# Pinning every engine but TensorE to source order in the seven-product stage of an encoder trunk

## The chip, the cores and the metric

The kernel runs on one core of a Trainium2 chip. The metric is the device time of one execution in microseconds (us). Engines are named as the profile names them: PE (TensorE matmuls), PEld (its weight loads), DVE (VectorE), ACT (ScalarE), POOL (GpSimd, here an issuer of DMAs) and SP (SyncE, which issues the other DMAs).

## The reference

Two requests, 512 and 256 tokens of width 1024 (768 columns together), pass through two layers. A layer is a mixer, a gated feed-forward part and a small embedding gate. The change lies in the feed-forward part, which is, cut short:

```python
def _conv_ffn(x, w_up, conv_w, conv_b, w_down):
    u = x @ w_up                                   # 1024 -> 2 * 2816
    up = jnp.pad(u, ((0, 0), (1, 1), (0, 0)))
    u = up[:, :-2] * conv_w[0] + up[:, 1:-1] * conv_w[1] + up[:, 2:] * conv_w[2] + conv_b
    a, gate = jnp.split(u, 2, axis=-1)
    return (a * jax.nn.gelu(gate, approximate=False)) @ w_down
```

All arithmetic is float32.

## The kernel before

Activations lie transposed: 128 features on the partitions, tokens along the free dimension. Float32 accuracy comes from splitting both operands of a matmul into a rounded high part and the low rest (`hi` by ACT, `lo = x - hi` by DVE), and from three matmuls: high by high, high by low, low by high.

`ffn` runs in three parts. The first 4 of the 22 blocks of 128 inner features are computed in the plain way (`proj`). The other 18 (`for j in range(NSTD, NF)`) form the seven-product stage: a block needs a 2 by 2 product of block matrices (two halves of the inner dimension, two halves of 384 tokens), and `seven` makes it with seven products in place of eight, from sums of weight blocks (S1 to S4) and of activations (N1, N2, T3, N4). The third part multiplies by `w_down`.

One iteration of the stage, in the order of the source (P1 to P7 are the products, twelve matmuls of 384 columns each; "step" is what `split_step` runs after the product):

- P1 = A11 B11. ACT copies it to `q1` (L184). Step: high and low part of S3 of this block.
- P2 = S1 N1. Step: high and low of S1 of the *next* block, then a POOL transfer into the same place.
- P3 = S2 N2. DVE: `u2` = P3 + q1 (L191), `g` = P2 + u2 (L192). Step: high and low of S4 of this block, then SP loads the pair of weight blocks after the next.
- P4 = S3 T3. DVE adds it and `g` into `us[1]` (L1081). Step: A11 of the next block, POOL transfer.
- P5 = A12 B21, summed onto P1's bank. ACT copies it to `us[0]` (L1083). Step: A12 of the next block, and a POOL transfer (L128) for the block after that.
- P6 = S4 B22, summed onto P2's bank, which `g` must have read. DVE adds (L1081). Step: S2 of the next block, POOL transfer.
- P7 = A22 N4, onto P4's bank. DVE adds (L1081). Step: A22 of the next block.

The sums S1, S2, S3, S4 of weights are made by transfers: POOL issues a DMA that adds a block of HBM onto the tile that holds the one before (L115 in `more`, L128). So S1, S2 and S4 of one block come one out of the other in the tile `ra`: load (L88), add, S1, add, S2, add, S4. The tile has two buffers, so the load for block j + 2 waits until S4 of block j is split. The high and low parts of one block pair share `whi` and `wlo` (two buffers), the others use `hs` and `ls` (three).

The convolution and gating of block j (`activate`) run during iteration j + 1: two Identity activations (L1028) at the end of iteration j, then one piece at each of the first five products: gate tap, gate tap, Gelu and a linear tap, a linear tap, and the product (DVE L1031, L1051; ACT L318).

The lines of `seven` on which most turns (`after` runs one piece of the convolution and one split step):

```python
        prod(y, "S2", "N2", True)
        nc.vector.tensor_tensor(out=u2, in0=y, in1=q1, op=ALU.add)
        nc.vector.tensor_tensor(out=g, in0=z, in1=u2, op=ALU.add)
        after()
```

Nothing but data dependences holds this order. A scheduler lays out each engine's instructions by its own estimate of when each is ready, with the source order as priority. Each engine then runs its queue strictly in the order laid out, and waits at the first instruction that isn't ready.

Of the kernel before, what the change touches and what calls it, by code (L numbers as in the profile page):

```python
# [45 lines left out]
class Net:  # L46
# [119 lines left out]
    def seven(self, c11, add):  # L166
        nc = self.nc
        X, W = self.X, self.pw.pop(0)

        def prod(bank, a, b, start):  # L170
            for n, ((wh, wl), (xh, xl)) in enumerate(zip(W[a], X[b])):
                for i, (w, v) in enumerate(((wh, xh), (wh, xl), (wl, xh))):
                    nc.tensor.matmul(bank, w, v, start=start and n == 0 and i == 0, stop=n == 3 and i == 2,  # L173
                                     skip_group_check=True)

        def after():
            self.tick()
            self.split_step()
        q1 = self.rp.tile([128, T], F32, tag="Rt", name="q1")[:, 0:HC]
        ug = self.rp.tile([128, T], F32, tag="sq", name="ug")  # L180
        u2, g = ug[:, 0:HC], ug[:, HC:T]
        x, z = self.mm()[:, 0:HC], self.mm()[:, 0:HC]
        prod(x, "A11", "B11", True)
        nc.scalar.copy(q1, x)  # L184
        after()
        prod(z, "S1", "N1", True)
        self.begin_split()
        after()
        y = self.mm()[:, 0:HC]
# [4 lines that stand above are left out]
        v = self.mm()[:, 0:HC]  # L194
        prod(v, "S3", "T3", True)
        add(1, 1, v, g)
        after()
        prod(x, "A12", "B21", False)
        c11(x)
        after()  # L200
        prod(z, "S4", "B22", False)
        add(0, 1, z, u2)
        after()
        prod(v, "A22", "N4", False)
        add(1, 0, v, u2)
        after()

# [779 lines left out]
    def ffn(self, l):  # L989
        nc, tc, a = self.nc, self.tc, self.a  # L990
        with tc.tile_pool(name=f"f{l}", bufs=1) as fp, \
# [43 lines left out]
            def activate(j, u, negated):  # L1035
                act[j] = aslot(j, f"act{j}", F32)
                if negated:
                    c = self.hp.tile([128, AC], F32, tag="h6", name="cg")
                else:
                    c = self.rp.tile([128, AC], F32, tag="sq", name="cg")  # L1040
                gbias = conv[:, NF + j, 3:4]
                gate = conv_taps(c, u[1], *((nconv, j, gbias) if negated else (conv, NF + j, gbias)))
                lin = conv_taps(act[j], u[0], conv, j, conv[:, j, 3:4])
                next(gate), next(lin)
                yield 1
                for _ in gate:
                    yield 1
                self.other(c, c, AF.Gelu)
                for _ in lin:
                    yield 1  # L1050
                nc.vector.tensor_tensor(out=act[j], in0=act[j], in1=c, op=ALU.mult)  # L1051

            def run(gen):
                for _ in gen:
                    pass
# [5 lines left out]
            for j in range(NSTD):  # L1061
                for part in range(2):
# [9 lines left out]
                    if part == 1:  # L1072
                        run(activate(j, us, False))
            self.drain()
            self.begin_split()
            for _ in range(6):
                self.split_step()
            for j in range(NSTD, NF):
# [6 lines left out]
                next(taps)  # L1085
                self.spawn(taps)
            self.drain()
            self.use_lnexp()
            for ph in range(2):
                accs = []  # L1090
# [281 lines left out]
```

## Time and profile before

| | |
|---|---|
| median of 3 runs | 2441.41 us (2431.51 to 2442.25) |
| the profiled execution, its own time | 2439.16 us |
| its span | 2437.4 us |
| PE busy, mean granted clock | 2313.6 us (95%), 0.981 |
| DVE, ACT, POOL busy | 1459.0, 1036.0, 193.3 us |
| first seven-product stage (layer 0) | 770.6 to 1103.6 us of the span |
| second one (layer 1) | 1814.8 to 2153.7 us of the span |

Busy shares are averages over stages; what the change is worth is read from the two stages. In the rows further down, a time in square brackets is how long the engine sat idle before the instruction and who ended that. The granted clock of PE has two levels, 1.00 (2.4 GHz) and 0.50 (1.2 GHz).

### The profile page before, as it was taken

The numbers are of one execution on the slowest core, as the hardware profiler recorded it, in microseconds if no ns is written. First come the engines' busy times: TensorE is split into PE (matmuls) and PEld (weight loads), VectorE is DVE, ScalarE is ACT, GpSimd is POOL, SyncE is SP. The second block draws the span as 40 slices with busy tenths as digits, with TensorE's granted clock in tenths as the row PEclk, the third lists the DMA queues.
The fourth block names the chain that finished last, engine by engine and source line by source line (L and its number), as shares of the span: only waits on it lengthen the run. The fifth ranks groups of instructions, "written<-read, shape, count | busy, mean of one in ns | idle before, by whom it ended". The sixth has DMA issues, their size and how long they took to land. (4 is left out here: it accounts for less than half of the span.)

```text
span 2437.4 us, 33498 instructions
## 1 busy us (share of the span) xinstructions
PE 2313.6 (95%) x13572; PEld 2098.2 (86%) x13572; DVE 1459.0 (60%) x2172; ACT 1036.0 (43%) x1506; POOL 193.3 (8%) x240
## 2 busy tenths in 40 slices
PE   7999999999999888889999999999998888899997
PEld 6989889898889878888888899998888887788887
DVE  7536364454568666665435687866596566664366
ACT  5333243323445334344335565545353343343353
POOL 1010010100002121110000000000021111200000
PEclk9999999999999999999999999999999999999999
DMA  4111111112336555553222211114265555531221
GB/s 158 52 53 44 53 44 44 52 44 85 110 102 133 117 110 115 109 106 102 67 74 81 97 53 36 41 38 136 100 136 114 108 106 115 101 118 61 74 87 52
DMA packets 85658, 208.74 MB, mean 86 GB/s; under 512 B 9632, under 2 KB 11680, under 8 KB 85504
## 3 DMA queue, kind: packets, MB, share of 16 engines
q1 hardware_dynamic: 60736, 162.03, 20.4%
q0 software_dynamic: 23616, 43.00, 11.7%
q8 instruction: 107, 1.75, 0.3%
q10 hardware_dynamic: 1152, 1.57, 0.2%
q14 instruction: 47, 0.39, 0.0%
HBM read 193.98 MB, written 12.58 MB: 85 GB/s over the span
## 5 line engine op out<-in xcount | busy, mean ns | idle before, releaser
L256 PE MATMUL pj<-xh,whi 128*128 128x512 f32 x2288 | 607.2, 346 | 9.1 <-ACT whi L73 6.0
L256 PE MATMUL pj<-xl,whi 128*128 128x512 f32 x2288 | 587.5, 338 | 3.5 <-DVE xl L312 3.5
L256 PE MATMUL pj<-xh,wlo 128*128 128x512 f32 x2288 | 585.7, 337 | 0.0
L256 PEld LDWEIGHTS pj<-xl,whi 128*128 128x128 f32 x2288 | 352.1, 188 | 56.0 <-DVE xl L312 5.3
L256 PEld LDWEIGHTS pj<-xh,whi 128*128 128x128 f32 x2288 | 351.1, 189 | 52.9 <-ACT whi L73 6.0
L256 PEld LDWEIGHTS pj<-xh,wlo 128*128 128x128 f32 x2288 | 349.7, 188 | 50.7
L73 ACT ACTIVATE whi<-raw 128x1024 fp32r<-128x1024 f32 (+2 forms) x182 | 181.0, 995 | 409.7 <-PE pj L256 391.5
L173 PE MATMUL mm<-x,whi 128*128 128x384 f32 x720 | 218.4, 371 | 93.6 <-DVE ug L192 90.8
L78 DVE TENSOR_TENSOR wlo<-raw,whi 128x1024 fp32r<-128x1024 f32 (+2 forms) x162 | 197.2, 1218 | 145.6 <-ACT whi L73 145.5
L173 PEld LDWEIGHTS mm<-x,whi 128*128 128x128 f32 x720 | 142.5, 207 | 106.4 <-DVE ug L192 101.2
L173 PE MATMUL mm<-x,wlo 128*128 128x384 f32 x432 | 155.5, 360 | 0.0
L110 ACT ACTIVATE whi<-ra 128x512 fp32r<-128x512 f32 x144 | 87.0, 628 | 119.7 <-DMA ra<-w_up 116.9
L173 PE MATMUL mm<-x,hs 128*128 128x384 f32 x432 | 123.0, 339 | 4.9 <-ACT q L184 4.9
L306 DVE TENSOR_TENSOR xl<-act,xh 128x772 fp32r<-128x772 f32 x88 | 83.5, 958 | 68.0 <-ACT xh L305 67.7
L115 POOL DMA_DIRECT2D ra<-w_up x108 | 104.5, 1154 | 245.1 <-DVE ls L111 188.5
L110 ACT ACTIVATE hs<-ra 128x512 fp32r<-128x512 f32 x36 | 22.7, 632 | 221.2 <-DMA ra<-w_up 209.6
L305 ACT ACTIVATE xh<-act 128x772 fp32r<-128x772 f32 x88 | 73.4, 841 | 96.8 <-PE pj L256 93.1
L111 DVE TENSOR_TENSOR ls<-ra,hs 128x512 fp32r<-128x512 f32 x36 | 24.9, 693 | 147.5 <-ACT hs L110 144.0
L111 DVE TENSOR_TENSOR wlo<-ra,whi 128x512 fp32r<-128x512 f32 x144 | 95.9, 687 | 17.3 <-ACT whi L110 16.6
L436 ACT COPY kc<-X 128x768 f32<-128x768 f32 x56 | 50.5, 902 | 124.5 <-PE mm L423 68.2
L173 PE MATMUL mm<-x,ls 128*128 128x384 f32 x288 | 97.1, 337 | 0.0
L111 DVE TENSOR_TENSOR ls<-rb,hs 128x512 fp32r<-128x512 f32 x72 | 49.5, 687 | 78.3 <-ACT hs L110 78.3
(276 smaller groups left out, 4023.7 us busy)
## 6 DMA issues: line engine op xcount, KB each, us to landing
ra<-w_up POOLq DMA_DIRECT2D x144, 256.0 KB, 4.7
raw<-w_ev SPq DMA_DIRECT2D x55, 512.0 KB, 3.5
raw<-w_dn SPq DMA_DIRECT2D x44, 512.0 KB, 3.5
rb<-w_up SPq DMA_DIRECT2D x72, 256.0 KB, 4.1
ra<-w_up SPq DMA_DIRECT2D x72, 256.0 KB, 3.4
raw<-w_od SPq DMA_DIRECT2D x24, 512.0 KB, 3.4
hd<-h SPq DMA_DIRECT2D x24, 384.0 KB, 2.3
h<-hd SPq DMA_DIRECT2D x24, 384.0 KB, 4.0
```

Source lines behind the costliest of these rows:

```text
L73: nc.scalar.activation(hi[:, s], raw[:, s], AF.Copy)
L78: nc.vector.tensor_tensor(out=lo[:, s], in0=raw[:, s], in1=hi[:, s].bitcast(F32), op=ALU.subtract)
L110: nc.scalar.activation(hi, r, AF.Copy)
L111: nc.vector.tensor_tensor(out=lo, in0=r, in1=hi.bitcast(F32), op=ALU.subtract)
L115: nc.gpsimd.dma_start(out=t, in_=src[n], accum_op=ALU.add)
L173: nc.tensor.matmul(bank, w, v, start=start and n == 0 and i == 0, stop=n == 3 and i == 2, skip_group_check=True)
L256: nc.tensor.matmul(o, w, x[:, c0:c0 + n], start=first and si == 0, stop=last and si == 2)
L305: nc.scalar.activation(xh[:, :n], src, AF.Copy)
L306: nc.vector.tensor_tensor(out=xl[:, :n], in0=src, in1=xh[:, :n].bitcast(F32), op=ALU.subtract)
L436: nc.scalar.copy(dst.rearrange("p (n c j) -> p n c j", c=2, j=h), src)
```

## The change

`ffn` notes how many instructions have been traced when the stage begins, and, when its last background work has been traced, calls `in_order`. That goes through the instructions traced between, and ties each to the one before it on the same engine by an edge that orders their issue and makes nothing wait for an end. PE is left out. So DVE, ACT, POOL and SP issue what belongs to the stage in the order of the source. No instruction is added, removed or resized. Work of the parts before and after the stage is not tied, and may still be laid out between.

```diff
+    def in_order(self, start):
+        last = {}
+        for i in list(self.nc.cur_bb.bb.instructions)[start:]:
+            if i.engine == mybir.EngineType.PE:
+                continue
+            if i.engine in last:
+                self.tc.add_manual_dep(i, last[i.engine].name, mybir.DependencyInfo(
+                    mybir.DependencyClass.NoSync, mybir.DependencyReason.DATA), reason="in_order")
+            last[i.engine] = i
...
             self.drain()
+            start = len(nc.cur_bb.bb.instructions)
             self.begin_split()
...
             self.drain()
+            self.in_order(start)
             self.use_lnexp()
```

## Rows read from the trace of the kernel before

**Rows 1.** The page: its span line and the line of engine busy time.

```profile
span 2437.4 us, 33498 instructions
PE 2313.6 (95%) x13572; PEld 2098.2 (86%) x13572; DVE 1459.0 (60%) x2172; ACT 1036.0 (43%) x1506; POOL 193.3 (8%) x240
```

**Rows 2.** Busy time by stretch: length of the stretch, then busy time (and instructions) of each engine, granted clock, mean busy share of the DMA engines, GB/s. The stretches are 170 us before the first stage, the first stage, what follows it, the second stage, and one single iteration.

```profile
600.00:770.00 170.00, 170.00 (x1001) 149.32 (x1000) 112.22 (x147) 80.79 (x111) 21.08 (x32) 1.00 0.41 113
770.60:1103.60 333.00, 284.16 (x1515) 276.59 (x1514) 211.15 (x343) 138.75 (x222) 59.65 (x68) 0.95 0.56 114
1103.60:1500.00 396.40, 396.40 (x2354) 348.98 (x2353) 231.50 (x283) 186.54 (x240) 0.00 (x0) 1.00 0.22 72
1814.80:2153.70 338.90, 289.21 (x1515) 280.50 (x1514) 211.19 (x343) 138.96 (x222) 59.68 (x68) 0.93 0.54 112
898.60:916.49 17.89, 15.00 (x87) 14.68 (x85) 11.65 (x19) 7.43 (x14) 3.53 (x4) 1.00 0.56 107
```

**Rows 3.** Groups of instructions by line, whole span: the two groups of the stage's matmuls before which PE sat idle. After the bar: busy time, mean ns of one, idle time before them and who ended it.

```profile
L173 PE MATMUL mm<-x,whi 128*128 128x384 f32 x720 | 218.4, 371 | 93.6 <-DVE ug L192 90.8 <-ACT u L1083 2.8
L173 PE MATMUL mm<-x,hs 128*128 128x384 f32 x432 | 123.0, 339 | 4.9 <-ACT q L184 4.9
```

**Rows 4.** Timeline of PE in one iteration: the first matmul of P3, the first of P5, the last of P5, the first of P6.

```profile
902.85 0.34 PE L173 MATMUL mm<-x,hs 128*128 128x384 f32 x1
...
907.02 0.51 PE L173 MATMUL mm<-x,hs 128*128 128x384 f32 x2
...
908.95 0.34 PE L173 MATMUL mm<-x,ls 128*128 128x384 f32 x1
912.18 0.62 PE L173 MATMUL mm<-x,whi 128*128 128x384 f32 x2 [2.89 <-DVE ug L192]
```

**Rows 5.** The same view as rows 2, of the matmuls right behind a longer stall of the first stage.

```profile
1023.60:1026.90 3.30, 3.30 (x12) 3.30 (x11) 0.58 (x3) 0.00 (x0) 0.00 (x0) 0.50 0.98 151
```

**Rows 6.** Timeline of DVE in the iteration of rows 4, from just after the end of P3.

```profile
905.02 0.69 DVE L111 TENSOR_TENSOR ls<-rb,hs 128x512 fp32r<-128x512 f32 x1 [2.43 <-ACT hs L110]
905.63 0.68 DVE L111 TENSOR_TENSOR wlo<-ra,whi 128x512 fp32r<-128x512 f32 x1
906.23 1.02 DVE L1031 SCALAR_TENSOR_TENSOR cg<-u,nconv,cg 128x772 f32<-128x772 f32 x1
907.16 1.02 DVE L1031 SCALAR_TENSOR_TENSOR act<-u,conv,act 128x772 f32<-128x772 f32 x1
908.10 1.02 DVE L1031 SCALAR_TENSOR_TENSOR cg<-u,nconv,cg 128x772 f32<-128x772 f32 x1
909.03 1.29 DVE L111 TENSOR_TENSOR wlo<-ra,whi 128x512 fp32r<-128x512 f32 x2
910.23 0.55 DVE L191 TENSOR_TENSOR ug<-mm,q 128x384 f32<-128x384 f32 x1
910.70 0.95 DVE L1051 TENSOR_TENSOR act<-act,cg 128x772 f32<-128x772 f32 x1
911.57 0.55 DVE L192 TENSOR_TENSOR ug<-mm,ug 128x384 f32<-128x384 f32 x1
```

**Rows 7.** Timelines of POOL, ACT and DVE (in the order of time) from there to the same place one iteration on.

```profile
909.61 0.86 POOL L128 DMA_DIRECT2D ra<-w_up  x1 [9.05 <-DVE cg L1031]
910.15 2.12 POOL L115 DMA_DIRECT2D ra<-w_up  x2
915.92 0.63 ACT L110 ACTIVATE hs<-ra 128x512 fp32r<-128x512 f32 x1 [5.41 <-DMA ra<-w_up]
916.58 0.69 DVE L111 TENSOR_TENSOR ls<-ra,hs 128x512 fp32r<-128x512 f32 x1 [3.33 <-ACT hs L110]
917.57 0.87 POOL L115 DMA_DIRECT2D ra<-w_up  x1 [5.30 <-DVE ls L111]
921.85 0.63 ACT L110 ACTIVATE whi<-ra 128x512 fp32r<-128x512 f32 x1 [2.91 <-DMA ra<-w_up]
923.64 0.68 DVE L111 TENSOR_TENSOR wlo<-ra,whi 128x512 fp32r<-128x512 f32 x1
927.05 1.28 DVE L111 TENSOR_TENSOR wlo<-ra,whi 128x512 fp32r<-128x512 f32 x2
```

**Rows 8.** The transfers by source line, whole span: duration of the issuing instruction in ns (min/median/max), and the time from issue to landing. L115 and L128 add onto `ra` from POOL, L88 is the plain load of `ra` by SP.

```profile
L115 POOL DMA_DIRECT2D ra<-w_up x108: 862/1214/1604, 766.4 to 2136.4; - x108
DMA to landing us min/median/max: 3.9/6.2/8.8
...
L128 POOL DMA_DIRECT2D ra<-w_up x34: 862/862/908, 763.3 to 2111.5; - x34
DMA to landing us min/median/max: 3.9/4.1/6.8
...
L88 SPq DMA_DIRECT2D ra<-w_up x36: 327/328/328, 749.7 to 2108.0; - x36
DMA to landing us min/median/max: 2.6/2.8/6.1
```

**Rows 9.** Groups of ACT's instructions in the iteration 898.60 to 916.49: the Identity that begins a gate.

```profile
L1028 ACT ACTIVATE cg<-u,conv,nconv 128x772 f32<-128x772 f32 x1 | 1.0, 1021 | 0.0
```

## The prediction

> **What bounds the kernel now.** I read the page first: PE is busy for 95% of the span [rows 1], so time can only come from PE's idle time or from slow matmuls. The busy time by stretch tells where those are: before the first stage and after it PE is busy all the time at a granted clock of 1.00, in the two stages it is busy for 284.16 of 333.00 and 289.21 of 338.90 us, at 0.95 and 0.93 [rows 2]. The groups by line name who ends the idle time: 93.6 + 4.9 = 98.5 us in both stages, 90.8 of it by L192, the `g` of each iteration [rows 3].
>
> What the stage would take without that is read from PE's timeline. P3 and P4 take 907.02 - 902.85 = 4.17 us [rows 4]; I take 2.095 us a product, so 7 x 2.095 = 14.67 us an iteration and 18 x 14.67 = 264.0 us a stage. The stages take 333.0 + 338.9 = 671.9 us, 18.66 an iteration. The excess is 671.9 - 528.0 = 143.9 us: 98.5 idle, and 45.4 of matmuls that run slowly. The slow ones follow the stalls: behind a stall of the first stage, twelve matmuls ran at 0.50, the lower of the two levels (1.2 GHz), and took 3.30 us in place of some 2.1 [rows 5]. Where nothing stalls, the clock stays at 1.00 [rows 2], so I let the 45.4 us go with the stalls.
>
> Why is `g` late? P3 ended at about 905.0, and P6 could have begun at 909.1, when P5's last matmul was issued (908.95) [rows 4]. But DVE had a high-low split, S4's low part, three taps and the low parts of S1 and A11 of the next block queued ahead of `u2`, and the last piece of the gate between `u2` and `g`; `u2` began at 910.23, `g` at 911.57 [rows 6], and P6 started 2.89 us late. This queue is itself part of a loop: the low parts at 909.03 release three POOL transfers; S2's high part waits for one until 915.92; its low part releases the next transfer at 917.57; S4 waits for that until 921.85; then S4's low part (923.64) and the taps; then S1 of the next block at 927.05, 18.02 us after 909.03 [rows 7]. S1 of the next block stands behind S4 of this one in DVE's queue, so two transfers lie in series in each iteration. That, not PE's work, is the period.
>
> **The change part by part.** No instruction is added or resized; each engine keeps its work and gets another order. The costs are therefore the waits that the new order makes. I lay an iteration out by the source, with time 0 at P1, products every 2.095 us (P2 ends at 4.2, P3 6.3, P4 8.4, P5 10.5, P6 12.6, P7 14.7), 0.1 us from an end to who waits for it, and DVE's issue spacing from its timeline: a low part 0.6, a tap 0.94, `u2` 0.47 [rows 6]; a high part 0.63 on ACT [rows 7], an Identity 1.02 [rows 9].
>
> *DVE.* From 0.1: the add behind the last P7 (0.5), A22's low part, a tap when its Identity is done (ACT: A22's high part until 0.8, Identity until 1.8, so 1.9 to 2.8), S3's low part when its high part is done (ACT: second Identity until 2.8, `q1` until 3.1, high part until 3.7; so until 4.4), the second tap until 5.3, S1's low part. S1's high part needs the `whi` half that P2 reads, so 4.3 to 4.9 on ACT, and the low part is done at 5.9. `u2` can then start as P3 ends, at 6.4; `g` is done at 7.4. P6 wants it at 10.5: 3.1 us early, where it is 2.9 late now. Behind it come a tap and S4's low part, done at 9.0, 1.5 us before P6: the tightest place. P4's adds, a tap, A11's low part and the gate's last piece reach 12.0, A12's low part 12.6, P6's adds 13.4, S2's low part 14.0 (P3 of the next iteration wants it at 18.9). DVE's work is 11.65 us an iteration [rows 2], under 14.67.
>
> *ACT* has 7.43 us [rows 2]; its waits are in the list above. *SP*'s load of the next pair follows S4's low part at 9.0; the loads of A12 and A22 ahead of it and behind it are wanted at 11 and 14.8.
>
> *POOL's transfers.* Now S1 of the next block comes ahead of S4 of this one, so the loop S1, S2, S4 no longer closes in one iteration. What is left is the loop of the tile `ra`, two iterations long: load, add, S1, add, S2, add, S4, load. From the end of S4's low part (905.63 + 0.68 = 906.31 [rows 6]) to the issue of the first add (909.61 [rows 7]) went 3.3 us, 2.8 of it the load's landing [rows 8]. Each high-low split takes from its landing to the next issue 917.57 - 915.92 = 1.65 us [rows 7]; three make 4.95. With *a* for an add from issue to landing the loop is 8.25 + 3a, and it stays under 2 x 14.67 = 29.3 up to a = 7.0. L128, issued first of a cluster, has a median of 4.1; L115 has 6.2 and at most 8.8 [rows 8], and behind L128 one landed some 5.7 after its issue (910.15 to 915.92 [rows 7]). In the source order the four adds of an iteration are issued at about 6.0, 11.2, 12.5 and 14.1, not three within 1.1 us, so I take a = 4.1 to 6.4: 20.6 to 27.5 us, under 29.3. The stages must move the same bytes in 0.79 of the time, so the DMA engines' share goes from 0.56 [rows 2] to about 0.70; that speaks for the upper half.
>
> *Beginning and end.* The first iteration has the splits of its own block ahead of `q1`, in one row, and DVE still owes the gate of the last plain block; before, the first two iterations stalled little. I take 3 us a stage, between 0 and 6 (about one product's 2.1 for a late S2 and the same for P6, each once, and a tail behind P7 of one high-low split, 1.65).
>
> **Sum.** 2439.16 - 143.9 + 2 x 3 = 2301.3 us. The profiled execution is 2.25 us under the median shown; I predict **2302 us**, with 2296 to 2308 for beginning and end alone.
>
> **The rivals.**
> *Late adds (faster, but less).* In the shorter iteration the adds land like the slowest now. At a = 7.5 the loop gives 15.4 us an iteration, 2302 + 36 x 0.73 = 2328; at 8.8, 17.3 and 2397. For it: L115's 8.8 and the fuller queues. Against it: those long landings come where three adds are issued in a row. Chance 0.13, half of it up to 2345.
> *Issues held by DVE.* DVE, busy for 11.65 us of 14.67 in place of 17.89 [rows 2], holds up POOL's issues. The longest issue lasted 1604 ns, the shortest 862 [rows 8]; 0.74 us more on each add of 6.4 makes a = 7.1, 14.8 us an iteration, 36 x 0.13 = 5 us: 2307. Against it: all 34 issues of L128 lasted 862 to 908 ns [rows 8], also where low parts were running on DVE (909.03 to 910.32, the issue at 909.61 [rows 6, 7]). Chance 0.02.
> The Trainium skill ("SBUF — State Buffer", "SBUF: two separate sides") has a harder form of this rule: a DVE instruction in a two-port mode keeps GpSimd from writing the descriptors of the DMAs it issues, 3100 ns in place of 620. With 2.5 us more on each add, an estimate from that page, a would be 8.9, the loop 17.5 us an iteration and the time 2404. The 862 to 908 ns of L128 don't agree with it.
> *Slower.* ACT and DVE now stand still at S1, S2, S3 and S4 until the add has landed, and everything behind, `u2` and `g` too, waits; before, a tap could be put ahead. The loop of `ra` then sets the pace, and it is slower than 18.66 from 8.25 + 3a = 37.3, a = 9.7 on. At a = 10 it is 19.1 us an iteration, 36 x 0.46 = 17 us: 2458. No add took over 8.8 [rows 8]. Chance 0.05.
> *No change.* The order of the other engines could be laid out as now where it matters, or P6 wait for something else than `g`: 2441. Against it: S4's low part was done at 906.3, well before P6 [rows 6], and `g` is the named releaser. Chance 0.03.
> *Part of the stall stays.* PE is not tied; it could be laid out with a later product first, or wait for a bank that `us[0]`'s copy frees (2.8 us now [rows 3]). A stall of 1.5 us an iteration makes 36 x 1.5 = 54, 2356, and up to twice that with the low clock. Chance 0.04.
> *The forecast*: 0.73, within 2291 to 2320.
>
> **How the numbers follow.** The range is 2291 (no cost at the ends, less the spread of runs) to 2345, which holds the forecast, the held issues and half of the late adds, 0.81. Half a per cent, 12 us, is about what a measurement of this kernel can tell from no change. Faster by more than that: forecast, late adds, held issues, partial stall, 0.92. Within: 0.03. Slower: 0.05.
>
> **What would show it.** In the profile after: both stages at 264 to 272 us, granted clock 1.00, PE's idle time before L173 under 10 us; DVE's timeline with `u2` and `g` side by side right behind P3 and two taps ahead of them, S4's low part behind; POOL's adds spread over the iteration, none over 7 us; everything outside the stages as it was. It is wrong if L173 still waits for L192 or for L111 in each iteration, if ACT's waits for `ra` push S4 past P6, or if the time gained in the stages comes back at the beginning of the part behind them.

## The result and the profile after

The changed kernel takes 2296.27 us (median of 3 runs, 2294.61 to 2297.43), against 2441.41 before: 0.9416 of the time, 95% interval 0.9378 to 0.9455. The profiled execution took 2297.43 us, 141.7 less than that of before.

The page's span and busy time, and the busy time by stretch (columns as in [rows 2]): the two stages, and one iteration of the first.

```profile
span 2295.7 us, 33373 instructions
PE 2270.6 (99%) x13572; PEld 2071.1 (90%) x13572; DVE 1463.9 (64%) x2172; ACT 1039.3 (45%) x1506; POOL 192.0 (8%) x240
```

```profile
771.60:1036.10 264.50, 264.50 (x1515) 264.50 (x1514) 212.63 (x341) 139.85 (x222) 59.01 (x68) 1.00 0.68 145
...
1747.30:2011.90 264.60, 264.60 (x1515) 264.59 (x1514) 212.09 (x341) 139.46 (x221) 58.95 (x68) 1.00 0.67 145
903.78:918.44 14.66, 14.66 (x85) 14.66 (x85) 11.83 (x19) 7.54 (x12) 3.43 (x5) 1.00 0.67 139
```

PE is busy through both stages at a granted clock of 1.00. They are 264.5 + 264.6 = 529.1 us long in place of 671.9 [rows 2]: 142.8 us, the whole difference between the two executions. The engines do the same work in it (DVE 212.63 us against 211.15). The groups by line show no idle time before the matmuls that had 98.5 us [rows 3]:

```profile
L173 PE MATMUL mm<-x,whi 128*128 128x384 f32 x720 | 196.4, 338 | 0.0
...
L173 PE MATMUL mm<-x,hs 128*128 128x384 f32 x432 | 121.7, 336 | 0.0
```

DVE's timeline in the iteration that begins at 903.78 (line numbers are 11 to 13 higher than before, except those of `seven` up to L192):

```profile
905.70 1.02 DVE L1042 SCALAR_TENSOR_TENSOR cg<-u,nconv,cg 128x772 f32<-128x772 f32 x1 [0.55 <-ACT cg L1039]
907.52 0.69 DVE L111 TENSOR_TENSOR wlo<-ra,whi 128x512 fp32r<-128x512 f32 x1 [0.79 <-ACT whi L110]
908.13 1.02 DVE L1042 SCALAR_TENSOR_TENSOR cg<-u,nconv,cg 128x772 f32<-128x772 f32 x1
909.06 0.69 DVE L111 TENSOR_TENSOR wlo<-ra,whi 128x512 fp32r<-128x512 f32 x1
910.27 0.56 DVE L191 TENSOR_TENSOR ug<-mm,q 128x384 f32<-128x384 f32 x1 [0.53 <-PE mm L173]
910.86 0.56 DVE L192 TENSOR_TENSOR ug<-mm,ug 128x384 f32<-128x384 f32 x1
911.34 1.01 DVE L1042 SCALAR_TENSOR_TENSOR act<-u,conv,act 128x772 f32<-128x772 f32 x1
912.27 0.68 DVE L111 TENSOR_TENSOR wlo<-ra,whi 128x512 fp32r<-128x512 f32 x1
```

Tap, S3's low part, tap, S1's low part; then DVE waits 0.53 us for P3, and `u2` and `g` run. Where seven instructions stood ahead of `u2` after P3's end [rows 6], there is none. `g` ends at 911.42, 7.6 us after P1's start, and P6 wants it at 10.5. POOL's adds of the iteration, and their landing (columns as in [rows 8]):

```profile
910.04 0.86 POOL L115 DMA_DIRECT2D ra<-w_up  x1 [5.79 <-DVE wlo L111]
915.31 0.86 POOL L115 DMA_DIRECT2D ra<-w_up  x1 [4.40 <-DVE wlo L111]
917.06 0.86 POOL L128 DMA_DIRECT2D ra<-w_up  x1 [0.89 <-DMA ra<-w_up]
918.07 0.86 POOL L115 DMA_DIRECT2D ra<-w_up  x1 [0.15 <-issue]
```

```profile
L115 POOL DMA_DIRECT2D ra<-w_up x108: 862/865/1217, 767.4 to 1996.6; - x108
DMA to landing us min/median/max: 3.6/4.6/7.4
...
L128 POOL DMA_DIRECT2D ra<-w_up x34: 862/865/1467, 768.6 to 1980.0; - x34
DMA to landing us min/median/max: 4.5/5.2/6.8
```

They are spread over the iteration; L115's median fell from 6.2 to 4.6 us, L128's rose from 4.1 to 5.2.

### The profile page after: what moved, and what is told of

It is laid out like the page before. It is cut to its first block, busy times and chain, and to the rows that moved or that the text cites. A ratio compares the mean times of both kernels' runs of the same rounds, so it can differ in the third digit from the quotient of the medians.

```text
span 2295.7 us, 33373 instructions
## 1 busy us (share of the span) xinstructions
PE 2270.6 (99%) x13572; PEld 2071.1 (90%) x13572; DVE 1463.9 (64%) x2172; ACT 1039.3 (45%) x1506; POOL 192.0 (8%) x240
## 4 chain that ended last, share of the span: by engine, by line
PE 97%; DVE 1%; ACT 0%; DMA 0%; issue 0%; POOL 0%; SPq 0%; DVEq 0%
PE pj L267 52%; PE mm L173 23%; PE mm L267 12%; PE mm L434 4%; PE mm L516 2%; PE mm L877 1%; PE mm L484 1%; PE mm L420 1%; PE mm L738 0%; PE mm L794 0%; PE mm L870 0%; DVE y L1192 0%; PE mm L397 0%; PE mm L475 0%; PE mm L529 0%; DMA xin<-xT 0%
## 5 line engine op out<-in xcount | busy, mean ns | idle before, releaser
L173 PE MATMUL mm<-x,whi 128*128 128x384 f32 x720 | 196.4, 338 | 0.0
L173 PE MATMUL mm<-x,wlo 128*128 128x384 f32 x432 | 145.7, 337 | 0.0
L173 PEld LDWEIGHTS mm<-x,whi 128*128 128x128 f32 x720 | 131.4, 188 | 0.1
L115 POOL DMA_DIRECT2D ra<-w_up x108 | 93.9, 874 | 391.3 <-DVE wlo L111 353.9
L111 DVE TENSOR_TENSOR wlo<-ra,whi 128x512 fp32r<-128x512 f32 x144 | 98.5, 685 | 27.0 <-ACT whi L110 27.0
L267 PE MATMUL mm<-xl,whi 128*128 128x512 f32 x352 | 90.5, 337 | 0.0
L267 PE MATMUL mm<-xh,whi 128*128 128x512 f32 x352 | 90.4, 337 | 0.0
L267 PE MATMUL mm<-xh,wlo 128*128 128x512 f32 x352 | 90.4, 338 | 0.0
```

Source lines behind the costliest of these rows:

```text
L111: nc.vector.tensor_tensor(out=lo, in0=r, in1=hi.bitcast(F32), op=ALU.subtract)
L115: nc.gpsimd.dma_start(out=t, in_=src[n], accum_op=ALU.add)
L267: nc.tensor.matmul(o, w, x[:, c0:c0 + n], start=first and si == 0, stop=last and si == 2)
```

## The experiments

The result fits two theories. *Loop*: S1 of the next block stood behind S4 of this one, so two adds lay in series in each iteration. *Queue*: `u2` and `g` stood behind other work in DVE's queue, and DVE's order alone decides. In both, the floor is the 14.67 us an iteration that PE's seven products take. Each experiment is given with the ratio to the kernel before, run beside it, and its 95% interval.

**Which engine's order matters.** Three kernels tie a part of the engines; in `in_order` only the condition differs.

```diff
-            if i.engine == mybir.EngineType.PE:
+            if i.engine != mybir.EngineType.DVE:                                   # e1
+            if i.engine != mybir.EngineType.Activation:                            # e2
+            if i.engine not in (mybir.EngineType.Pool, mybir.EngineType.SP):       # e4
```

*ACT alone.* Expected:

> Only ACT is tied to the source order. DVE's queue, laid out by the scheduler, then has S1's low part ahead of S4's, but both linear taps and S4's low part ahead of g, which in the source stand behind it. Loop: the loop is open, and g, with two taps (1.9 us) and a low part (0.6) more ahead of it, is done at about 9.2 after P1, before P6 at 10.5: the whole gain, 2296 to 2305 us. Queue: DVE isn't tied, g still stands behind five taps and low parts, so most of the stall stays: 2380 to 2441.

Measured: 2295.68 us, 0.9426 [0.9397, 0.9455]: the whole gain. DVE's timeline of one iteration around `g`:

```profile
908.25 0.69 DVE L111 TENSOR_TENSOR wlo<-ra,whi 128x512 fp32r<-128x512 f32 x1
908.85 1.02 DVE L1042 SCALAR_TENSOR_TENSOR act<-u,conv,act 128x772 f32<-128x772 f32 x1
909.78 0.55 DVE L191 TENSOR_TENSOR ug<-mm,q 128x384 f32<-128x384 f32 x1
910.25 0.68 DVE L111 TENSOR_TENSOR wlo<-ra,whi 128x512 fp32r<-128x512 f32 x1
910.85 0.55 DVE L192 TENSOR_TENSOR ug<-mm,ug 128x384 f32<-128x384 f32 x1
```

S1's low part (908.25) stands ahead of S4's (910.25), because ACT makes the high parts in that order and DVE's layout follows. Both linear taps and S4's low part are ahead of `g`, and nothing is lost. So `g` need not be next to P3, and DVE, POOL and SP need no tie. The adds no longer leave in a cluster of three here either (L115's median is 4.8 us), so this run alone doesn't tell the place of S1 from the spread of the adds.

*DVE alone.* Expected:

> Only DVE is tied to the source order. Two theories. Loop: before, the period of 18 us is the loop S1, add, S2, add, S4, taps, S1 of the next block, because S1's low part stands behind S4's on DVE; any order that opens the loop, or makes it shorter than PE's 14.67 us, gives the whole gain. Queue: u2 and g stand behind other work on DVE, whatever the transfers do, so DVE's order alone decides. Both expect the whole gain here: 2296 to 2305 us. A third, that ACT's and POOL's order count as much, expects a part of it: 2340 to 2400.

Measured: 2322.39 us, 0.954 [0.9511, 0.957]. Both theories expected the whole gain, and 26 us are missing; the third expected 2340 or more, so none of the three has it. It isn't `g` that PE waits for, but two low parts: P6 for S4's (first line) and, in other iterations, P4 for S3's (second).

```profile
L173 PE MATMUL mm<-x,wlo 128*128 128x384 f32 x432 | 148.1, 343 | 10.6 <-DVE wlo L111 10.1
...
L173 PE MATMUL mm<-xb,wlo 128*128 128x384 f32 x36 | 13.6, 378 | 8.7 <-DVE wlo L111 8.7
```

POOL's and ACT's timelines of one iteration in which P6 waits:

```profile
911.88 0.86 POOL L128 DMA_DIRECT2D ra<-w_up  x1 [1.59 <-DMA ra<-w_up]
912.42 1.22 POOL L115 DMA_DIRECT2D ra<-w_up  x1
```

```profile
917.85 0.63 ACT L110 ACTIVATE whi<-ra 128x512 fp32r<-128x512 f32 x1 [1.69 <-DMA ra<-w_up]
...
918.74 0.63 ACT L110 ACTIVATE whi<-ra 128x512 fp32r<-128x512 f32 x1
```

ACT, not tied, takes S4's high part (917.85), `q1`, and then S1's (918.74), while DVE is bound to S1, `u2`, `g` and a tap before S4. The add that makes S4 leaves right behind L128 (912.42) and lands 5.4 us later, which is what ACT waits for. A stage takes 279.6 and 281.9 us, 15.6 an iteration. An order on one engine that contradicts the order on another costs what the two together make wait.

*POOL and SP alone.* Expected:

> Only POOL and SP are tied; DVE and ACT keep the order of the kernel before. POOL's add for the block after next (L128) then goes behind the adds for S2 and S3 and no longer ahead of them. Loop: the add after S1 lands as the first of its cluster, in about 4.1 us and not 5.7, so the period falls by 1.6 to 1.7 us, to 16.3 or 16.4; over 36 iterations, with some of the low clock gone, 60 to 80 us less than before: 2360 to 2380. Queue: nothing that stands ahead of g on DVE has moved, 2430 to 2442.

Measured: 2354.71 us, 0.9668 [0.9642, 0.9694]. The stages by stretch and POOL's timeline:

```profile
769.50:1063.60 294.10, 272.02 (x1515) 266.68 (x1514) 211.16 (x343) 138.63 (x222) 59.67 (x68) 0.99 0.61 130
1774.80:2069.40 294.60, 271.64 (x1515) 266.32 (x1514) 211.25 (x343) 138.72 (x222) 59.66 (x68) 0.99 0.61 130
```

```profile
908.37 1.75 POOL L115 DMA_DIRECT2D ra<-w_up  x2 [9.55 <-DVE wlo L111]
909.68 1.33 POOL L128 DMA_DIRECT2D ra<-w_up  x1
```

L128 goes behind both L115; L115's landing has a median of 4.2 us and L128's 6.5. POOL and SP were not tied apart from each other. The period is 588.7 / 36 = 16.35 us, as the loop expects, with DVE's queue as before. The time is a little under the range given: with the shorter stalls, 272.0 + 271.6 - 528.0 = 15.7 us of the 45.4 us of slow matmuls are left, less than I had allowed. Queue expected no change and falls: before, the work ahead of `g` was late because of the adds. What is left of the stall is still `g`'s (45.0 us of PE's idle time in both stages).

**S1 behind S4, with `u2` and `g` in front.** The changed kernel with one step of `split_pair` moved.

```diff
         a12 = self.load_block(src[1])
+        yield
         parts("S1", s, 0, 0)
         more(s, 0)
-        yield
         a22 = self.load_block(src[3])
         yield
```

> The changed kernel, but the split of S1 of the next block moved one step later in the source, so that it stands right behind S4 of this block on ACT and DVE, as in the kernel before; u2 and g stay right behind P3. The loop S1, S2, S4 closes in one iteration again. Loop, by its length: three splits of 1.65 and two adds of 4.6 to 4.8 make 14.2 to 14.6 us, just under 14.67: 2296 to 2315. If it were the place of S1 behind S4 as such, as the prediction puts it, the period would go back towards 18: 2400 or more. Queue: g is where it was, 2296 to 2300.

Measured: 2358.08 us, 0.9683 [0.9656, 0.971]; the stages take 291.7 and 293.0 us, 16.2 an iteration. None of the three cases came out. PE waits for S3's high part (P4). The group with P4's first matmuls, ACT's timeline, and the next add:

```profile
L173 PE MATMUL mm<-xb,whi 128*128 128x384 f32 x216 | 70.9, 355 | 29.7 <-ACT whi L110 29.7
```

```profile
905.83 0.63 ACT L110 ACTIVATE hs<-ra 128x512 fp32r<-128x512 f32 x1 [4.61 <-DMA ra<-w_up]
...
909.97 0.63 ACT L110 ACTIVATE whi<-ra 128x512 fp32r<-128x512 f32 x1
912.29 0.85 ACT L329 ACTIVATE cg<-cg 128x772 f32<-128x772 f32 x1 [1.69 <-DVE cg L1042]
913.05 1.66 ACT L110 ACTIVATE whi<-ra 128x512 fp32r<-128x512 f32 x3
```

```profile
915.89 0.86 POOL L115 DMA_DIRECT2D ra<-w_up  x1 [7.54 <-DVE wlo L111]
```

S2's high part waits 4.61 us at the head of ACT's queue for its add; S3's (909.97), the Gelu and S4, S1 and A11 (913.05) stand behind it; S1's low part releases the next add at 915.89, 10.06 us after 905.83. That add shares the transfer engines with SP's loads, issued just before it (914.88 to 915.73); L115's median here is 5.8 us. So there is a loop of one iteration with a single add in it, through ACT's queue, which neither I nor either theory had: S2, the rest of ACT's queue, S1, add, S2. Moving S1 one step earlier, as the changed kernel has it, takes Gelu and S4 out of it.

**Two loops, lengthened on purpose.** In both kernels a block of weights is added more often than once, so the weight sums and all that follows aren't the reference's; times are read, not values.

```diff
         more(s, 0)
+        more(s, 0)
+        more(s, 0)
```

> The changed kernel with the add that makes S2 out of S1 issued three times in a row, so S2 and what is added onto it later aren't the reference's. Each further add waits for the landing of the one before, 4.1 us on POOL plus 0.2. The prediction's loop, that of the tile ra over two iterations, 8.25 + 3a with a of 4.6 to 5.2 as measured after the change, goes from 22.7 to 31.3: 15.7 us an iteration, 36 us more than the 2296 us of the changed kernel, 2332. Rival: a loop of one iteration that the prediction left out. S2's high part waits on ACT for the add; behind it stand A22's high part, both Identities, q1 and S3's and S1's high parts, then S1's low part on DVE and the add again: by the changed kernel's trace 6.5 us from S2's high part to the issue, and the adds. With three adds that is 6.5 + 3 x 4.3 = 19.4 us, 4.7 more than PE's 14.67: 2296 + 170 = 2466, or up to 2490 with the low clock.

Measured: 2534.28 us, 1.04 [1.0375, 1.0425]; a stage takes 382.1 us, 21.2 an iteration. The loop of `ra` (15.7) falls, the loop through ACT is what binds. POOL's timeline (the last line is the add that begins the next three) and the end of ACT's wait:

```profile
956.01 0.86 POOL L115 DMA_DIRECT2D ra<-w_up  x1 [4.81 <-DVE wlo L111]
960.15 0.86 POOL L115 DMA_DIRECT2D ra<-w_up  x1 [3.28 <-DMA ra<-w_up]
965.47 1.76 POOL L115 DMA_DIRECT2D ra<-w_up  x2 [4.45 <-DMA ra<-w_up]
...
976.92 0.87 POOL L115 DMA_DIRECT2D ra<-w_up  x1 [4.67 <-DVE wlo L111]
```

```profile
969.44 0.63 ACT L110 ACTIVATE hs<-ra 128x512 fp32r<-128x512 f32 x1 [8.55 <-DMA ra<-w_up]
```

Three adds took 969.44 - 956.01 = 13.4 us (12.9 expected), and the rest of a period was not 6.5 but 976.92 - 969.44 = 7.5 us: 20.9 us in place of 19.4. That is why the time lies above the 2490 given. In this iteration nothing on the way from S2's high part to the next add waits for PE, so the granted clock of 0.89 isn't seen to lengthen the loop. In the changed kernel, with one add of 4.1 to 4.6, this loop has 11.5 to 12 us, under 14.67.

```diff
             after, _, t = self.ploads[0]
             nc.gpsimd.dma_start(out=t, in_=after[3], accum_op=ALU.add)
+            nc.gpsimd.dma_start(out=t, in_=after[3], accum_op=ALU.add)
```

> The changed kernel with the add of L128 (the one that makes S1's tile for the block after next) issued twice, so the sums of weights aren't the reference's. The loop of ra over two iterations goes from 22.7 to 28.0 us, still under 29.3: no change, 2296 to 2300 us. Rival: a loop through POOL's queue in one iteration. S4's low part releases the load (3.3 us with its issue), the add of L128 is issued 0.85 later and waits in POOL's queue ahead of the add that makes S4 out of S2; that one lands 5.35 us after its issue and S4 is split (1.4 us). With one add that is some 12.5 us, under 14.67; a second one, that waits for the landing of the first (5.2 us), makes 17 to 17.5: 36 x 2.4 to 2.8, so 2380 to 2400 us, more with the low clock.

Measured: 2402.41 us, 0.9856 [0.9837, 0.9875]; the stages take 315.1 and 318.0 us, 17.6 an iteration. The loop of `ra` would have allowed it at no cost; the loop through POOL's queue gives 17 to 17.5. POOL's timeline (L129 is the second add), and ACT's behind it:

```profile
912.98 0.86 POOL L128 DMA_DIRECT2D ra<-w_up  x1 [1.45 <-DMA ra<-w_up]
918.05 0.86 POOL L129 DMA_DIRECT2D ra<-w_up  x1 [4.21 <-DMA ra<-w_up]
918.98 0.86 POOL L115 DMA_DIRECT2D ra<-w_up  x1
```

```profile
922.14 0.63 ACT L110 ACTIVATE whi<-ra 128x512 fp32r<-128x512 f32 x1 [4.78 <-DMA ra<-w_up]
...
924.42 1.15 ACT L110 ACTIVATE whi<-ra 128x512 fp32r<-128x512 f32 x2 [0.90 <-DMA ra<-w_up]
```

The add that makes S4 of this block (918.98) waits in the queue behind an add for a later one. Without the second add the loop is 17.6 - 5.1 = 12.5 us. The run lengthens another way round as well, which its expectation doesn't have: S1's high part (922.14) waits 4.78 us for the doubled add itself, and the Gelu and S4's high part stand behind it on ACT. S4's add is the later of the two by only 0.90 us (924.42). So a loop of about 12.5 us through the load and L128 is shown, but POOL's queue alone isn't shown to be what closes it.

**Is `g`'s place enough by itself?** The changed kernel with `u2`, `g` and P4's adds behind the pieces that follow P5.

```diff
         prod(y, "S2", "N2", True)
-        nc.vector.tensor_tensor(out=u2, in0=y, in1=q1, op=ALU.add)
-        nc.vector.tensor_tensor(out=g, in0=z, in1=u2, op=ALU.add)
         after()
         v = self.mm()[:, 0:HC]
         prod(v, "S3", "T3", True)
-        add(1, 1, v, g)
         after()
         prod(x, "A12", "B21", False)
         c11(x)
         after()
+        nc.vector.tensor_tensor(out=u2, in0=y, in1=q1, op=ALU.add)
+        nc.vector.tensor_tensor(out=g, in0=z, in1=u2, op=ALU.add)
+        add(1, 1, v, g)
```

> The changed kernel, but u2, g and the adds of P4 come in the source behind the pieces that follow P5, so DVE has a linear tap, S4's low part, another tap, A11's low part, the gate's last piece and A12's low part ahead of them. The transfers keep their order and their time. If g's place in DVE's queue is enough to stall P6, whatever the transfers do: A12's high part follows P5 (10.5) on ACT, its low part ends at 12.5, g at 13.5, 3 us after P6 could begin; 17.6 us an iteration, 2296 + 36 x 3 = 2404, up to 2430 with the low clock. If only the loop through the transfers counts: 2296 to 2300.

Measured: 2353.23 us, 0.9657 [0.9634, 0.9679], between the two cases, and not a clean test: PE isn't tied, and the scheduler put P1 and a part of P2 of the next block ahead of P6. What PE waits for is then the copy of P5, whose bank P1 takes:

```profile
910.18 0.63 PE L173 MATMUL mm<-x,whi 128*128 128x384 f32 x2 [1.00 <-ACT u L1095]
```

So I tied PE as well (`in_order` without the lines that skip PE), with `g` late and, as the control, alone.

> As e8_g_late, but PE is tied to the source order too, so P6 can't be put behind products of the next block. If g's place in DVE's queue is enough: the copy of P5 ends at 11.0, A12's high part at 11.6, its low part at 12.4, u2 and g at 13.5, and P6 starts 3.0 to 3.1 us late in each iteration: 17.7 us, 2296 + 36 x 3 = 2404, up to 2440 with the low clock. If the loop through the transfers is needed: 2296 to 2300.

> The changed kernel with PE tied to the source order too: the control for e9_g_late_pe_tied. PE ran P1 to P7 in that order in the changed kernel already, so no change: 2294 to 2299 us.

Measured: the control takes 2297.05 us, 0.9423 [0.9403, 0.9442], no change against the changed kernel. With `g` late it is 2448.33 us, 1.0054 [1.0036, 1.0072]: the whole gain is gone, and a little more. The group of P6's matmuls and DVE's timeline:

```profile
L173 PE MATMUL mm<-x,whi 128*128 128x384 f32 x720 | 216.4, 368 | 103.1 <-DVE ug L199 103.1
```

```profile
913.30 0.69 DVE L111 TENSOR_TENSOR ls<-rb,hs 128x512 fp32r<-128x512 f32 x1 [1.84 <-ACT hs L110]
913.91 0.55 DVE L198 TENSOR_TENSOR ug<-mm,q 128x384 f32<-128x384 f32 x1
914.50 0.56 DVE L199 TENSOR_TENSOR ug<-mm,ug 128x384 f32<-128x384 f32 x1
```

DVE stands idle for 1.84 us before A12's low part with `u2` ready behind it. L115's median is 4.1 us here, so no late add is in it. 103.1 / 36 = 2.86 us of stall an iteration, and the stages take 342.9 and 341.3 us. The time is above the 2440 given because slow matmuls cost more than I had allowed: PE is busy for 579.8 us in both stages, 579.8 - 528.0 = 52 us over the floor, at 0.93. A late `g` is enough by itself, then. In the kernel before, it was late through the adds; here through its place. That place is a later one than before, though: behind A12's low part, which needs the copy of P5, where before A12's low part came after `g`. That the old place alone would stall P6 isn't shown.

## Why the prediction was right, point by point

- *What bounds the kernel.* 14.67 us an iteration as the floor: measured 14.66. All the 143.9 us of excess, the slow matmuls with the idle time, were to go: 142.8 went, and the clock is 1.00 in both stages.
- *The layout of an iteration.* With 903.78 as 0, `u2` starts at 6.5 (6.4 in the working), `g` ends at 7.6 (7.4), S4's low part ends at 9.2 (9.0).
- *Why `g` is late.* The working puts S1's place behind S4 down to DVE's queue. ACT's queue held the same order, S4's high part at 921.85 [rows 7] and S1's at 924.19:

```profile
924.19 1.15 ACT L110 ACTIVATE whi<-ra 128x512 fp32r<-128x512 f32 x2
```

Tying ACT alone undid it. And the low parts at 909.03 released two transfers, not three: L128 was issued at 909.61, before the first of them had ended (909.72); what it had waited for was more likely the load of its tile, which S4's low part had released.

- *The adds.* a between 4.1 and 6.4: medians 4.6 and 5.2. The longest is 7.4, over the 7 that I gave. The DMA engines' share is 0.68 and 0.67 (0.70).
- *Beginning and end.* The term that was mis-sized: 3 us a stage, measured 264.5 - 264.0 = 0.5 us. The sum with 0.5 in its place is 2296.3 for the profiled execution, which took 2297.43.
- *The loop that is left.* This step failed, with no effect on the number. I had the tile `ra` over two iterations as the only loop, with room up to a = 7.0. Two loops of one iteration, one through ACT's queue and one through L128 and its load, are nearer: some 11.5 to 12 and 12.5 us against 14.67, where that of `ra` has 22.7 us for two iterations. The second leaves some 2 us, for a load and an add together. Nothing in the working bounded them; that they stayed under PE's time was luck.
- *"That, not PE's work, is the period."* Half right. The adds in series set the period before (16.35 us with one of them shorter), but S1 behind S4 cost 1.5 us an iteration, not 4, once `g` was in front, and `g` late by its place costs all of it with no add late.
- *The change itself.* I costed all four engines' order. ACT's alone gives the whole gain of some 140 us, DVE's alone 113 us of it, POOL's and SP's alone 81.
- *The rivals.* Late adds, the slower case, no change and a stall that stays did not come up. Issues held by DVE: with DVE busy for 212.63 of 264.50 us, L115's issue has a median of 865 ns, lower than before (1214). The Trainium skill's rule on this ("SBUF — State Buffer", "SBUF: two separate sides") is about DVE instructions in a two-port mode, and the same section says that `tensor_tensor`, which makes the low parts, `u2` and `g` here, has no such mode. So for most of DVE's work the prediction's 2404 took the rule further than it goes; the 865 ns agree with the section.

## What to carry to other kernels

Where a TensorE-bound stage stalls, follow the waits round until they close, and write down every loop with the number of iterations it spans; a transfer that stands at the head of an in-order queue puts all that is behind it into the loop, other blocks' work too. A scheduler that lays out by its own estimate of readiness can place work of the next block on the wrong side of a wait; tying one engine to a software-pipelined source order may be enough (here ACT, which makes the high parts, and whose order DVE's layout followed). A tied order is only as good as the source: with `u2`, `g` and P4's adds in the wrong place and PE tied too, the kernel took 2448.33 us, 0.5% more than the untied one.

## What the runs showed of the hardware that I had not expected

How long an add took to land went with what left beside it more than with the load on the DMA engines: at a share of 0.68 L115's median was 4.6 us, at 0.56 it was 6.2; L128 had 4.1 as the first of three and 6.5 as the last. With S1 behind S4, at a share of 0.61, L115 had 5.8, and the add followed there left right behind SP's loads.

And the stalls of PE cost more than their length, since matmuls behind them run slowly: 36 stalls of 1.25 us in the mean (45.0 us, POOL and SP tied) went with 15.7 us of slow matmuls at a granted clock of 0.99, 36 of 2.86 us with 52 us at 0.93. The clock isn't all of it. With S1 behind S4, PE is idle for 33.4 us and busy for 551.3 - 528.0 = 23.3 us over the floor, again at 0.99, and a clock lower by 0.01 makes some 6 us of 584.7 (an estimate). Some of the rest are P4's matmuls that wait for S3's low part: the 36 of `xb` and `wlo` have a mean of 433 ns there, 336 in the changed kernel. What makes up the remainder no run shows.
